# A hybrid MLA and NSA decoder block on one core: moving two norm chains, and holding filler work on three more engines to its place

## The chip, the core and the metric

The kernel runs on one core of a Trainium2 chip. A core has a TensorE (PE) for matmuls, VectorE (DVE), ScalarE (ACT) and GpSimd (POOL) for elementwise work, and SyncE (SP), which here issues the weight loads. Each engine takes its instructions in a fixed order, and semaphores make one wait for another. The metric is the device time of one execution in microseconds.

## The reference

One decoder layer over 512 tokens with 1024 channels, in float32. A normed and modulated `h` is multiplied with one wide matrix `w_in`, whose columns feed two attentions (multi-head latent attention, MLA, and native sparse attention, NSA) and their gates; a gated feed-forward part follows.

```python
h = rms_norm(x, norm1_gain[l]) * (1.0 + sc1) + sh1
z = h @ w_in[l]
(c_q, c_kv, k_pe, q_n, k_c, v_c, k_s, v_s, k_w, v_w,
 g_nsa, g_mla_merge, g_nsa_merge) = jnp.split(z, split_at, axis=-1)
y_mla = mla_attention(c_q, c_kv, k_pe, ...) @ w_o_mla[l]
y_nsa = nsa_attention(q_n, k_c, v_c, k_s, v_s, k_w, v_w, g_nsa, ...) @ w_o_nsa[l]
merged = jax.nn.sigmoid(g_mla_merge) * y_mla + jax.nn.sigmoid(g_nsa_merge) * y_nsa
x = x + gt1 * (merged @ w_out[l])
h2 = rms_norm(x, norm2_gain[l]) * (1.0 + sc2) + sh2
x = x + gt2 * ((jax.nn.silu(h2 @ ffn_w_gate[l]) * (h2 @ ffn_w_up[l])) @ ffn_w_down[l])
```

Two norms of the NSA part matter here:

```python
q = partial_rope(rms_norm(q, q_gain), cos_t, sin_t)               # queries, 8 heads of 64
kc = compress(k_c, cmp_pos_k, cmp_w1_k, cmp_w2_k)                 # compressed keys, 31 blocks x 2 groups
kc = partial_rope(rms_norm(kc, kc_gain), ...)
```

In the NSA scores three softmaxes are added with learned gates: over the compressed keys, over selected blocks and over a window of 256.

## The kernel before, in words

Every large product is split: a float32 matrix becomes a high part (`whi`, `hTh`, `phi`, `KH`), written by ScalarE, and the rest (`wlo`, `hTl`, `plo`, `KL`), by VectorE or GpSimd, and three matmuls make one product. A weight chunk is loaded by SP into `raw` and split into `whi` and `wlo`; `feed.prep(n)` does that for chunk n.

The stages, by the trace: the first products with `w_in` to some 65 us; the rest of `w_in` in a strict order to 152 us; NSA heads to 300; the MLA latents to 345; MLA heads to 440; then output products and the feed-forward part to the end at 871.

**The strict part.** There `Paced.strict` chains each engine's instructions in the order in which the code emits them. Generators are advanced by hand, `steps(gen, n)` one and `emit(...)` several. `cols_products(j)` (j = 0 to 11) issues the matmuls `ga` of 352 columns of `w_in`, four chunks to a set of four PSUM tiles, which `keep_cols` copies to `zA`, two on ScalarE and two on VectorE. Between them stand:
- `tq` (turn_q): turned queries, evacuated as `QS` in two halves by ScalarE and VectorE from the PSUM tile `pq`;
- `nq` (norm_rows of the queries): its first four steps sum squares into `msq`; its last step is a chain of 12 small VectorE operations of 128x32 from `msq` to `rs_n`, the reciprocal root norm of every token and head. The NSA scores are the first to read `rs_n`;
- `outs["k"]` (compress_out of the keys): the first step squares the compressed keys on ScalarE (`kcd`, `sk`), runs a chain on VectorE (`sk`, the `rq_..._kc` operations, `kcr`, `rp_kc`) and copies the result to `kcd`; the second step transposes `kcd` on TensorE; the third splits it to `KH` and `KL`;
- `blocks["v"]` (compress_blocks): transposes `ZC` on TensorE and copies them to `X` on ScalarE (three) and VectorE (one), after GpSimd has cleared a part of `X`;
- `pk` (prep_k): keys, split to `KH`/`KL`; `w1`, `w2`: the two small layers of the compression (`FS`, `hid`, `hidT`, `po`); `prep_gates`, `rope` work on GpSimd.

**The heads.** Outside of the strict part a scheduler, which simulates a timeline when the kernel is built, picks each engine's order from what the code emits. NSA works in eight units (tile t of 128 queries, group g of four heads): `nsa_scores` makes, for each head, window and compressed scores (`pw`), selected ones (`ps`), and on VectorE `cm`, `s` and the negated maxima `mn`, then exponentials on ScalarE; at its end four `s` are multiplied by `sm` on VectorE and four on GpSimd. Each `pw` needs the PSUM tile that the `mn` before it freed. `nsa_values` transposes (`pt`), splits (`phi`, `plo`) and multiplies (`av`). MLA has eight heads of the same kind.

Beside this main work stand fills, advanced by `Side.tick` through `later()`, or marked by `as_filler`: the merge gates (`gates_gen`, 88 steps in NSA: each step is three matmuls `gp`, eight steps one chunk with two `whi` and two `wlo`; two chunks are made ahead, in the strict part), `latent_stats` (`jk` on ScalarE, `kpr` on VectorE, `kB` on GpSimd), the modulation rows (`macc` on VectorE), and in the MLA stage the rest of the gates and `w_o_nsa` (`yn`, `gs`). In NSA the gates' `wlo` run on GpSimd, later on VectorE.

A wrapper `Paced` around each engine records the main line in `log`. When an engine's `pace` is positive, a fill on it must follow the main-line instruction that lies `pace` places back:

```python
if not Paced.fill:
    self.log.append(ins)
elif len(self.log) >= self.pace > 0:
    self.follow(ins, self.log[-self.pace])
```

Before the change only TensorE has a pace (16 in NSA, 24 in MLA).

Of the kernel before, what the change touches and what calls it, by code (L numbers as in the profile page):

```python
# [29 lines left out]
BRIDGE = 12  # L30
PACE_D = 16
PACE_F = 24
FILL_LEAD = 1
FILL_CUT = 2
YM_AHEAD = 1
# [81 lines left out]
def hybrid_block(ctx, tc, a, out):  # L117
# [47 lines left out]
    pe, act, dve, pool, sp = (Paced(e) for e in (nc.tensor, nc.scalar, nc.vector, nc.gpsimd, nc.sync))  # L165
# [153 lines left out]
    def steps(gen, n):  # L319
        for _ in range(n):  # L320
            if next(gen, "end") == "end":
                break
# [47 lines left out]
    def with_side(gen):  # L370
        for _ in gen:
            side.tick()
# [689 lines left out]
    rq, tq, rk, pk = rope_q(), turn_q(), rope_k(), prep_k()  # L1062
    blocks, w1, w2, outs = ({nm: f(i, nm) for i, nm in (K, V)} for f in (compress_blocks, compress_w1, compress_w2, compress_out))
    nk, nq = norm_rows(UK, 4, "k", rs_k), norm_rows(UQ, 8, "q", rs_n)

    def emit(*todo):
        for gen, n in todo:
            steps(gen, n)
# [107 lines left out]
    cols_products(1)  # L1176
    emit((w2["k"], 2), (tq, 1))
    feed.prep(18)
    steps(tq, 1)
    steps(nq, 1)  # L1180
    steps(outs["k"], 1)
    cols_products(2)
    steps(blocks["v"], 1)
    feed.prep(19)
# [37 lines left out]
    cols_products(9)  # L1222
    emit((w2["v"], 1), (pk, 1))
    feed.prep(29)
    emit((pk, 2), (w2["v"], 1))
    cols_products(10)
    steps(w2["v"], 2)
    steps(pk, 1)
# [151 lines left out]

    with tc.tile_pool(name="nat", bufs=2, side="right", reuse_waits="tile") as nat:
        pe.pace = PACE_D
        spill_src.update(pool=nat, bufs=2)
        units = [(t, g) for t in range(NT) for g in range(2)]
        states = [[] for _ in units]
        nb = lambda u: 1 + units[u][0] + 1 + min(units[u][0] + 1, 3) + 1
        stats = latent_stats(nat)
        side.start(5 * len(units) + sum(nb(u) for u in range(len(units))), (gates_gen, D_GATES), (stats, 8), (mods_gen, D_MODS))
        act.gate, dve.gate, pool.gate = act.last, dve.last, pool.last
        with_side(nsa_scores(nat, *units[0], states[0]))  # L1390
        for u in range(len(units)):
            pairs = [(nsa_values(nat, *units[u], states[u]), nb(u))]
            if u + 1 < len(units):
                pairs.append((nsa_scores(nat, *units[u + 1], states[u + 1]), 5))
            with_side(mix(*pairs))
    act.gate = dve.gate = pool.gate = None
    nsa_last = pe.log[-1]
    spill_src.clear()
    pe.pace = 0
    fill_on[0] = dve  # L1400
    tab_st.close()

# [217 lines left out]

    with tc.tile_pool(name="mat", bufs=2, side="right", reuse_waits="tile") as mat:
        pe.pace = PACE_F
        spill_src.update(pool=mat, bufs=GS_BUFS)
        sl = [[] for _ in range(NH)]
        side.start(12 * NH - 4, (chain(gates_gen, yn_gen), F_FILL), (mods_gen, F_MODS))
        with_side(mla_scores(mat, 0, qk[0], sl[0]))
        for h in range(NH):
            pairs = [(mla_values(mat, h, sl[h]), 5)]
            if h == 0:
                pairs.append((as_filler(norm_q(1)), 1))  # L1630
            if h + 1 < NH:
                pairs.append((mla_scores(mat, h + 1, qk[h + 1], sl[h + 1]), 5))
            if h + 2 < NH:
                pairs.append((mla_heads(h + 2, qk[h + 2]), 2))
            if h == NH - 1:
                y_gen = y_mla(0)
                pe.pace = PACE_Y
                pairs.append((as_filler(part(y_gen, 3)), 3))
            with_side(mix(*pairs))
        mla_last = pe.log[-1]  # L1640
        pe.pace = 0
        run(gates_gen)
        run(yn_gen)
    pe.gate = mla_last
# [403 lines left out]
```

## Time and profile before

| what | value |
|---|---|
| median of 3 runs | 871.19 us (871.17 to 871.99) |
| the profiled execution, its own time | 873.04 us |
| its span in the trace | 871.3 us |
| mean granted clock of TensorE | 0.986 of 2.4 GHz |
| TensorE busy | 844.3 us (97%) |
| VectorE busy | 674.9 us (77%) |
| ScalarE busy | 456.0 us (52%) |
| GpSimd busy | 109.3 us (13%) |
| chain of work that ended last: TensorE, VectorE | 81%, 7% |

A timeline row has the start, the busy time, the engine and line (L153 is the wrapper's line, so all rows have it), the operation, output and input tiles with their shapes, how many rows are merged, and in brackets how long the engine had been idle and who ended that. Busy times on one engine overlap a little, since the next instruction starts while one drains. The granted clock is 1.00 at 2.4 GHz and 0.50 at 1.2 GHz; a value between is a mean over a window.

### The profile page before, as it was taken

To read this page: it belongs to the slowest core of one execution; us is meant where nothing else is said; L and a number is where in the kernel's file an instruction comes from. 1 tells how busy PE (TensorE), PEld (TensorE's weight loads), DVE (VectorE), ACT (ScalarE), POOL (GpSimd) and SP (SyncE) were. 2 spreads that over 40 slices of the span, in tenths; PEclk is the share of its full clock that TensorE was granted. 3 is DMA by queue.
4 is the path that set the end of the run, shared out by engine and by line. 5 is a ranking of instruction groups with operands and counts; after the bars stand their busy time and mean duration, and the time that the engine had idled before them with its cause. 6 is when DMAs were issued, how large, how long until landed. Compare 5 with 4: busy or idle time off the path is not lost.

```text
span 871.3 us, 13969 instructions
## 1 busy us (share of the span) xinstructions
PE 844.3 (97%) x5060; PEld 745.1 (86%) x5060; DVE 674.9 (77%) x1391; ACT 456.0 (52%) x960; POOL 109.3 (13%) x199
## 2 busy tenths in 40 slices
PE   8999989799999999899999999999999999999997
PEld 8889889677877789787888889898999889988996
DVE  5878777888987478688789877986887858965875
ACT  4756635577766567664633254552466226641550
POOL 0007400534441013112200000000000000000000
PEclk9999989699999999999999999999999999999999
DMA  9934546343201124334697753443233313332312
GB/s 310 364 115 150 156 137 175 100 117 97 76 24 58 45 84 125 111 96 164 181 324 249 255 159 104 141 146 97 73 98 121 123 50 115 104 125 91 98 49 97
DMA packets 95705, 115.54 MB, mean 133 GB/s; under 512 B 6564, under 2 KB 68884, under 8 KB 95636
## 3 DMA queue, kind: packets, MB, share of 16 engines
q1 hardware_dynamic: 92596, 108.32, 40.1%
q10 hardware_dynamic: 2400, 4.23, 1.3%
q0 software_dynamic: 640, 2.10, 0.6%
q8 instruction: 40, 0.66, 0.3%
q14 instruction: 29, 0.24, 0.1%
HBM read 106.24 MB, written 8.39 MB: 132 GB/s over the span
## 4 chain that ended last, share of the span: by engine, by line
PE 81%; DVE 7%; ACT 3%; issue 3%; POOL 2%; DMA 2%; SPq 1%; ACTq 0%; DVEq 0%; POOLq 0%
PE d L153 14%; PE fx L153 12%; PE fy L153 9%; PE gp L153 8%; PE pt L153 4%; PE ga L153 4%; PE av L153 3%; PE yn L153 3%; PE gwo L153 3%; PE fg L153 3%; PE gym L153 3%; PE fu L153 3%; PE wo L153 3%; PE gq L153 2%; PE ps L153 2%
## 5 line engine op out<-in xcount | busy, mean ns | idle before, releaser
L153 ACT ACTIVATE whi<-raw 128x1024 fp32r<-128x1024 f32 (+4 forms) x159 | 141.1, 905 | 128.9 <-PE d L153 48.2
L153 DVE TENSOR_TENSOR wlo<-raw,whi 128x1024 fp32r<-128x1024 f32 (+4 forms) x140 | 150.9, 1086 | 56.4 <-ACT whi L153 52.4
L153 PE MATMUL d<-wlo,mh 128*128 128x512 f32 (+1 forms) x180 | 70.2, 390 | 0.0
L153 PE MATMUL d<-whi,mh 128*128 128x512 f32 (+1 forms) x180 | 69.6, 391 | 0.6 <-DVE tm L153 0.5
L153 ACT ACTIVATE s<-s,mn 128x384 f32<-128x384 f32 (+3 forms) x96 | 52.5, 547 | 28.4 <-DVE mn L153 28.3
L153 PE MATMUL d<-whi,ml 128*128 128x512 f32 (+1 forms) x180 | 67.3, 389 | 0.0
L153 DVE TENSOR_TENSOR plo<-pt,phi 128x512 fp32r<-128x512 f32 (+2 forms) x78 | 46.2, 602 | 17.8 <-ACT phi L153 17.5
L153 ACT ACTIVATE phi<-pt 128x512 fp32r<-128x512 f32 (+2 forms) x78 | 39.9, 524 | 29.3 <-PE pt L153 28.6
L153 PE MATMUL gp<-hTh,whi 128*128 128x512 f32 x128 | 54.5, 425 | 0.0
L153 PE MATMUL gp<-hTh,wlo 128*128 128x512 f32 x128 | 51.2, 400 | 0.0
L153 PE MATMUL gp<-hTl,whi 128*128 128x512 f32 x128 | 50.9, 398 | 0.0
L153 ACT ACTIVATE whi<-s 128x1024 fp32r<-128x1024 f32 (+1 forms) x36 | 30.1, 845 | 30.7 <-PE d L153 18.0
L153 PE MATMUL fx<-h2h,whi 128*128 128x256 f32 x144 | 41.2, 286 | 0.0
L153 PEld LDWEIGHTS d<-whi,mh 128*128 128x128 f32 x180 | 33.7, 188 | 8.8 <-DVE tm L153 1.2
L153 PE MATMUL fx<-h2h,wlo 128*128 128x256 f32 x144 | 40.9, 284 | 0.0
L153 PE MATMUL fx<-h2l,whi 128*128 128x256 f32 x144 | 40.8, 283 | 0.0
L153 PEld LDWEIGHTS d<-whi,ml 128*128 128x128 f32 x180 | 33.8, 188 | 7.7
L153 PEld LDWEIGHTS d<-wlo,mh 128*128 128x128 f32 x180 | 33.8, 188 | 7.4
L153 DVE TENSOR_TENSOR wlo<-s,whi 128x1024 fp32r<-128x1024 f32 (+1 forms) x36 | 33.7, 950 | 7.4 <-ACT whi L153 7.4
L153 PE MATMUL pt<-ident,s 128*128 128x128 f32 x232 | 37.4, 278 | 0.1
L153 PE MATMUL ga<-whi,hTh 128*128 128x352 f32 x96 | 32.8, 341 | 2.3 <-DVE zA L153 2.3
L153 PEld LDWEIGHTS pt<-ident,s 128*128 128x128 f32 x232 | 28.1, 142 | 7.4 <-issue 1.9
(433 smaller groups left out, 2668.0 us busy)
## 6 DMA issues: line engine op xcount, KB each, us to landing
raw<-in_ada_w_dram SPq DMA_DIRECT2D x23, 512.0 KB, 4.5
raw<-in_ffn_w_gate_dram SPq DMA_DIRECT2D x22, 512.0 KB, 3.8
raw<-in_ffn_w_up_dram SPq DMA_DIRECT2D x22, 512.0 KB, 4.0
raw<-in_ffn_w_down_dram SPq DMA_DIRECT2D x22, 512.0 KB, 3.8
araw<-in_ada_w_dram SPq DMA_DIRECT2D x32, 256.0 KB, 6.5
raw<-in_w_in_dram SPq DMA_DIRECT2D x16, 512.0 KB, 4.7
strip<-in_ada_w_dram SPq DMA_DIRECT2D x9, 512.0 KB, 3.8
raw<-in_w_in_dram SPq DMA_DIRECT2D x12, 352.0 KB, 4.0
```

The source lines that it names most:

```text
L153: out = call(*args, **kw)
```

## The change

It has three parts. The first step of `outs["k"]` moves ahead of the last step of `tq`. The last step of `nq` leaves that place and comes after chunk 29 is split, ahead of `cols_products(10)`. And a constant `PACE_E = 4` gives a pace to ScalarE, VectorE and GpSimd in the NSA heads, and to ScalarE and VectorE in the MLA heads.

```diff
+PACE_E = 4
@@ strict part, between cols_products(1) and cols_products(2)
     emit((w2["k"], 2), (tq, 1))
     feed.prep(18)
+    steps(outs["k"], 1)
     steps(tq, 1)
-    steps(nq, 1)
-    steps(outs["k"], 1)
     cols_products(2)
@@ between cols_products(9) and cols_products(10)
     emit((w2["v"], 1), (pk, 1))
     feed.prep(29)
-    emit((pk, 2), (w2["v"], 1))
+    emit((pk, 2), (w2["v"], 1), (nq, 1))
     cols_products(10)
@@ NSA heads
         pe.pace = PACE_D
+        act.pace = dve.pace = pool.pace = PACE_E
...
-    pe.pace = 0
+    pe.pace = act.pace = dve.pace = pool.pace = 0
@@ MLA heads
         pe.pace = PACE_F
+        act.pace = dve.pace = PACE_E
...
-        pe.pace = 0
+        pe.pace = act.pace = dve.pace = 0
```

What it does to the order of instructions is shown at three places. First VectorE in the strict part, around chunk 18. The names are those above; `X_1` is the values' `X`. Before:

```order
L153 TENSOR_TENSOR QS_790<-pq_1375,QS_790 64x4x128
L153 TENSOR_TENSOR QS_791<-pq_1375,QS_791 64x4x128
L153 TENSOR_SCALAR msq<-msq 128x32
...
L153 SCALAR_TENSOR_TENSOR rs_n<-rq_m_nq,rq_i_nq 128x32
L153 TENSOR_SCALAR sk<-sk 64x1
...
L153 SCALAR_TENSOR_TENSOR kcr<-po,sk,g_n 64x64
...
L153 COPY kcd<-kcr 64x64 x2
L153 TENSOR_TENSOR wlo<-raw,whi 128x1024
L153 COPY X_1_1456<-pt 64x511
```

and after:

```order
L154 TENSOR_TENSOR wlo<-raw,whi 128x704
L154 TENSOR_SCALAR sk<-sk 64x1
...
L154 SCALAR_TENSOR_TENSOR kcr<-po,sk,g_n 64x64
...
L154 COPY kcd<-kcr 64x64 x2
L154 TENSOR_TENSOR QS_790<-pq_1375,QS_790 64x4x128
L154 TENSOR_TENSOR QS_791<-pq_1375,QS_791 64x4x128
L154 TENSOR_TENSOR wlo<-raw,whi 128x1024
L154 COPY X_1_1441<-pt 64x511
```

The key norm stands ahead of the two `QS`, the query norm is gone from here, and the rest follows unchanged. On ScalarE the squares for `kcd` likewise move ahead of its two `QS`; TensorE's order in the strict part is the same.

Second, VectorE at the end of the strict part (`hidT` and `VC` belong to the values' compression). Before:

```order
L153 TENSOR_TENSOR kd_1832<-UK_210,rs_k 128x512
L153 COPY hidT_1834<-pt 128x128
L153 TENSOR_TENSOR wlo<-raw,whi 128x1024
L153 TENSOR_TENSOR KL<-pk_1863,KH 128x2x128 x2
L153 TENSOR_TENSOR VC<-vt_1877,VC 32x64
...
L153 COPY zA_794<-ga_1732 128x352
L153 COPY zA_796<-ga_1734 128x352
```

and after:

```order
L154 TENSOR_TENSOR kd_1817<-UK_210,rs_k 128x512
L154 COPY hidT_1819<-pt 128x128
L154 TENSOR_SCALAR msq<-msq 128x32
...
L154 SCALAR_TENSOR_TENSOR rs_n<-rq_m_nq,rq_i_nq 128x32
L154 TENSOR_TENSOR wlo<-raw,whi 128x1024
L154 TENSOR_TENSOR KL<-pk_1863,KH 128x2x128 x2
L154 TENSOR_TENSOR VC<-vt_1877,VC 32x64
...
L154 COPY zA_794<-ga_1717 128x352
L154 COPY zA_796<-ga_1719 128x352
```

The 12 operations of the query norm stand between `hidT` and the `wlo` of chunk 30.

Third, VectorE at the start of the NSA heads, from the last `zA` on. An `ISA` row with `s` is a score with its minimum, the `ISA mn` behind it reads the minimum out. Before:

```order
L153 COPY zA_796<-ga_1734 128x352
L153 SCALAR_TENSOR_TENSOR cm<-pw,rs_n,consts 128x32
L153 ISA s_1937,mn<-pw,consts,rs_n 128x128
...
L153 ISA s_1945,mn<-ps,mask,rs_n 128x128
...
L153 TENSOR_TENSOR kpr<-zA_793,g_k 128x32
L153 SCALAR_TENSOR_TENSOR macc<-raw,csil,macc 128x512
L153 TENSOR_TENSOR kpr<-zA_794,g_k 128x32
...
L153 SCALAR_TENSOR_TENSOR macc<-raw,csil,macc 128x512
L153 SCALAR_TENSOR_TENSOR cm<-pw,rs_n,consts 128x32
L153 ISA s_1951,mn<-pw,consts,rs_n 128x128
```

and after:

```order
L154 COPY zA_796<-ga_1719 128x352
L154 SCALAR_TENSOR_TENSOR cm<-pw,rs_n,consts 128x32
L154 ISA s_1937,mn<-pw,consts,rs_n 128x128
...
L154 ISA s_1945,mn<-ps,mask,rs_n 128x128
...
L154 SCALAR_TENSOR_TENSOR cm<-pw,rs_n,consts 128x32
L154 ISA s_1951,mn<-pw,consts,rs_n 128x128
...
L154 ISA s_1959,mn<-ps,mask,rs_n 128x128
...
L154 SCALAR_TENSOR_TENSOR cm<-pw,rs_n,consts 128x32
L154 ISA s_1969,mn<-pw,consts,rs_n 128x128
...
L154 TENSOR_SCALAR s_1937<-s_1937,sm 128x128
```

Before, four `kpr` and two `macc` stand between the first score and the second; after, the first four scores follow one another, and the first `macc` and `kpr` come behind the multiplications of `s`. On ScalarE four `whi` stood ahead of the first exponential; after, two of them come after the twelve exponentials of the first six scores. On GpSimd four `wlo` stood ahead of the first multiplications of `s`; after, two come behind these. TensorE's order is the same up to the sixth score; then the seventh `pw` and `ps` come after the first transposes of `s`. At the start of the MLA heads two `whi` and a `gs` no longer stand ahead of a `phi` on ScalarE, and four `wlo` no longer ahead of the first scores on VectorE. SP loads some chunks of `w_o_nsa` one place earlier. From 440 us on, all orders are as before.

## Rows read from the trace of the kernel before

**Rows 1.** The page, part 1: busy time, share, instructions of each engine, whole span.

```profile
PE 844.3 (97%) x5060; PEld 745.1 (86%) x5060; DVE 674.9 (77%) x1391; ACT 456.0 (52%) x960; POOL 109.3 (13%) x199
```

**Rows 2.** Waits of TensorE: us in total, times, longest us.

```profile
PE pw L153 <- DVE mn L153: 5.1, 4, 3.6
...
PE av L153 <- ACT phi L153: 2.8, 5, 1.6
...
PE ga L153 <- DVE zA L153: 2.3, 1, 2.3
PE pt L153 <- DVE kcd L153: 2.0, 1, 2.0
```

**Rows 3.** Windows: length, busy us (instructions) by engine, granted clock, DMA share, GB/s.

```profile
110.00:120.00 10.00, 7.71 (x34) 7.42 (x33) 6.62 (x13) 2.59 (x4) 0.00 (x0) 0.66 0.48 143
155.00:175.00 20.00, 15.59 (x61) 12.65 (x59) 16.09 (x60) 10.18 (x39) 9.43 (x13) 0.66 0.41 119
225.00:250.00 25.00, 24.72 (x121) 18.86 (x119) 23.06 (x74) 19.93 (x56) 9.19 (x12) 1.00 0.21 64
350.00:360.00 10.00, 7.70 (x40) 5.68 (x39) 7.87 (x25) 7.11 (x18) 2.54 (x7) 1.00 0.29 98
400.00:410.00 10.00, 8.66 (x42) 6.91 (x41) 7.59 (x17) 5.48 (x15) 1.89 (x2) 0.83 0.48 169
```

**Rows 4.** Timeline of VectorE, strict part: start us, busy us, instruction, count, [idle before].

```profile
101.17 1.39 DVE L153 TENSOR_TENSOR QS<-pq,QS 64x512 fp32r<-64x512 f32 x2 [0.30 <-ACT QS L153]
102.59 0.18 DVE L153 TENSOR_SCALAR msq<-msq 128x32 f32<-128x32 f32 x1
...
105.69 0.14 DVE L153 TENSOR_SCALAR sk<-sk 64x1 f32<-64x1 f32 x1
...
107.82 0.28 DVE L153 SCALAR_TENSOR_TENSOR kcr<-po,sk,g_n 64x64 f32<-64x64 f32 x1
...
108.80 0.29 DVE L153 COPY kcd<-kcr 64x64 f32<-64x64 f32 x2
...
110.25 0.69 DVE L153 COPY X<-pt 64x511 f32<-64x511 f32 x1
...
112.28 0.96 DVE L153 COPY zA<-ga 128x352 f32<-128x352 f32 x2
```

**Rows 5.** Timeline of ScalarE, strict part.

```profile
106.38 1.80 ACT L153 ACTIVATE X<-pt 64x512 f32<-64x512 f32 x3 [2.66 <-POOL X L153]
108.20 0.82 ACT L153 ACTIVATE zA<-ga 128x352 f32<-128x352 f32 x2
```

**Rows 6.** Timeline of ScalarE, last w_in part.

```profile
149.35 0.38 ACT L153 ACTIVATE KH<-pk 128x256 fp32r<-128x256 f32 x1 [0.49 <-DVE KL L153]
...
150.88 0.46 ACT L153 ACTIVATE zA<-ga 128x352 f32<-128x352 f32 x1 [0.59 <-PE ga L153]
```

**Rows 7.** Timeline of TensorE, start of the NSA heads.

```profile
152.10 0.39 PE L153 MATMUL gp<-hTh,whi 128*128 128x512 f32 x1
...
159.67 0.47 PE L153 MATMUL pw<-KH,QS 128*128 128x160 f32 x1 [3.56 <-DVE mn L153]
```

**Rows 8.** Timeline of VectorE, start of the NSA heads.

```profile
153.44 0.80 DVE L153 TENSOR_TENSOR kpr<-zA,g_k 128x32 f32<-128x32 f32 x1
154.16 1.83 DVE L153 SCALAR_TENSOR_TENSOR macc<-raw,csil,macc 128x512 f32<-128x512 f32 x1
...
158.35 0.74 DVE L153 SCALAR_TENSOR_TENSOR macc<-raw,csil,macc 128x512 f32<-128x512 f32 x1
159.01 0.24 DVE L153 SCALAR_TENSOR_TENSOR cm<-pw,rs_n,consts 128x32 f32<-128x32 f32 x1
...
159.72 0.07 DVE L153 DVE_READ_ACCUMULATOR2_ANT mn<- 128x1 f32 x1
...
168.80 1.01 DVE L153 TENSOR_SCALAR s<-s,sm 128x128 f32<-128x128 f32 x4
```

**Rows 9.** Timeline of GpSimd, start of the NSA heads.

```profile
152.89 5.49 POOL L153 TENSOR_TENSOR wlo<-raw,whi 128x512 fp32r<-128x512 f32 x4 [46.55 <-DVE zA L153]
```

## The prediction, made before the changed kernel ran

> **What bounds the kernel now.** I read the page's busy shares first: TensorE is busy for 97% of the span [rows 1], so only its stops and its slow stretches can be won. The list of TensorE's waits [rows 2] has stops at three places. In the strict part it waits 2.0 us for `kcd` and 2.3 us for `zA`, once each. At the start of the NSA heads one `pw` waits 3.6 us for `mn`. The waits of `av` for `phi` sum to 2.8 us and lie mostly in the MLA heads. Then the windows [rows 3]: the granted clock averages 0.66 over 110 to 120 us, which is 6.8 us at half rate, and 0.66 over 155 to 175 us, which is 13.6 us at half. Both begin at stops. In 350 to 360 us TensorE stops for 2.3 us and keeps the full clock; in 400 to 410 it stops for 1.3 us and has 0.83. So a stop of this size may or may not cost the clock. I treat the clock as a term of its own.
>
> **Strict part.** Nothing is added or removed; 12 operations (the query norm, from `msq` at 102.59 to `sk` at 105.69, 3.10 us) leave VectorE's queue here, and the key norm (105.69 to the end of `kcd` at some 109.0, 3.3 us) moves ahead of the two `QS` copies [rows 4]. These edits issue no DMA, so no queue of transfers is passed.
> The key norm can then start where `QS` began to wait, 101.17 − 0.30 = 100.87. Its `kcr` came 107.82 + 0.28 − 105.69 = 2.41 us after its start, so it will be done at 103.28, and `kcd` at 104.2. TensorE asks for `kcd` at 107.2 (its 2.0 us wait ended just past 109.0), so that wait goes. There is a small new one: the transposes of the values' blocks now take the PSUM bank that `kcr` frees, where they took the one that `QS` freed at 102.56. That is 0.7 us later, and TensorE reaches `kcd` at 107.9.
> What is late next is ScalarE's `zA`. It stands behind three `X` copies, which wait for GpSimd until 106.38 and end at 108.18; the first `zA` ends near 108.6 [rows 5]. So TensorE stops for 0.7 to 0.9 us there. VectorE's own `X` waits for the same ScalarE copies. Before, `X` began at 110.25 and `zA` at 112.28, 2.03 us later [rows 4]; after, `X` begins at 108.2 and `zA` at 110.23. The matmuls behind that `zA` start **2.05 us earlier**. The gain cannot be the 4.3 us of the two waits, since `X` is not moved.
> The clock: of 6.8 us at half rate at most 2.3 lie in the stop, so at least 4.5 are matmuls that lose half, 2.25 to 3.4 us. I price it at **2.5 us if the clock stays up**. The new stops (0.7, 0.9, 0.7) are shorter but lie closer together.
>
> **Start of the NSA heads.** The query norm's 3.10 us now stand on VectorE ahead of the last `wlo`. ScalarE's second `KH` waited for VectorE's `KL` [rows 6]; VectorE had 0.43 us to spare there, so `KH` moves from 149.35 to about 152.0. From there to the first `zA` ScalarE needs 150.88 − 0.59 − 149.35 = 0.94 us plus 0.46 for the copy: 153.4. The first gate matmul, at 152.10 before [rows 7], waits for that `zA`: a **new stop of 1.3 us** (bounds: 0, if the norm fits in other pauses, and 3.1, all of it).
> TensorE ran from 152.10 to its stop at 159.67 − 3.56 = 156.11, 4.0 us; the same work now ends at 157.4. Before, four `kpr` and two `macc` lay between VectorE's first and second score, from 153.44 to 159.01, 5.57 us [rows 8]. They are fills, and the pace moves them behind later scores; a score itself takes 159.79 − 159.01 = 0.78 us. The second score now ends as soon as TensorE delivers it, at about 157.9, and the third starts there instead of at 159.67.
> From 159.67 to the multiplications of `s` (168.80) it took 9.1 us for the scores up to the seventh, with two `macc` among them. After, the seventh score stands behind the multiplications, and the `macc` are gone. At half clock I take 8.0 us: 165.9, a gain of 2.9. At full clock a score takes 0.78 us on VectorE and some 0.4 on TensorE, since each `pw` waits for the `mn` before: four of them 4.8, and the row of small sums 0.7, 163.4, a gain of 5.4. Full clock also gives 1.8 us from 168.8 to 172.5, the rest of the 13.6 us at half. The seventh score is only put off and costs 0.4 later. So **2.5 us if the clock still falls, 6.8 if it doesn't**.
>
> **The put-off fills.** The 5.57 us of `kpr` and `macc` must be done later. VectorE is busy for 23.06 of 25 us in 225 to 250 [rows 3], and there a fill can come ahead of a score again. Ends: 0 if every one finds a pause, 5.57 if all of them show on TensorE. In that window TensorE stopped for only 0.28 us although VectorE was 92% full, so I stay near the low end: **−1.2 us**.
> The rows say how these fills are priced: the `macc` of 154.16 took 1.83 us while GpSimd ran its four `wlo`, until 158.38 [rows 9], and that of 158.35 took 0.74. The Trainium skill, page "SBUF — State Buffer", section "Who interferes with whom", has a rule for it: a VectorE instruction with two SBUF inputs contends with a GpSimd instruction that reads SBUF, and the one that starts first blocks the other. The trace agrees (1.83 against 0.74). By it the fills would shrink once they no longer lie beside those `wlo`, the term would be nearer −0.6 and the forecast 0.6 us lower; but the same `wlo` now run beside other work, and I leave it.
>
> **MLA heads.** ScalarE's weight copies and a `gs` no longer stand ahead of a `phi`, and VectorE's four `wlo` go from before the first scores. At stake: stops of 2.3 us in 350 to 360, and in 400 to 410 stops of 1.3 us and 1.7 us by the clock (17% of ten), 5.3 us in all. Bounds 0 and 5.3; the fills have to go somewhere here as well, with TensorE's `yn` matmuls behind them, so I take **+1.5 us**. From 440 us on, the order is as before: 0.
>
> **The sum.** Without the clock: 2.05 + 2.5 + 1.5 − 1.2 = 4.85 us. The clock's two terms are 2.5 and 4.3; I expect one of the two stretches to stay up, and take their mean, 3.4. That gives 8.25 us. The profiled execution took 873.04 us by its own time (span 871.3), so 864.8 on that scale; the median of the runs was 871.19, 1.85 lower, and there it is **862.9 us**.
>
> **Rivals.**
> *Both slow stretches remain* (chance 0.25). The stops shrink but TensorE is still idle between scores, and the clock fell in 400 to 410 us after only 1.3 us of stops [rows 3]. Then 4.85 us: 866.3. The Trainium skill, page "TensorE: Matmul & The Clock Gate", Part 1, says that the throttled clock is the default and that activity releases it; sparse scores would then stay slow, which is this rival. The trace bears it out only half: 350 to 360 us, with 2.3 us of stops, kept its clock.
> *Both stay up, and most MLA stops close* (0.20): 2.05 + 2.5 + 6.8 + 1.5 − 1.2 = 11.65 with the MLA term as it is, 859.5; with 5 us of it, 856.0.
> *Slower* (0.12). Held fills starve the gate matmuls. Each gate chunk needs two `wlo` on GpSimd, 2 × 1.37 = 2.74 us [rows 9]. Before, four of them ran ahead of anything else; now GpSimd first does four multiplications of `s`, and a later chunk's third matmul stands behind a `wlo` that was made just before. Nine of the eleven chunks are made in this stage. If each costs half of its pair, 1.3 us, that is 11.7 us: 871.19 − 8.25 + 11.7 = 874.6. It decides from 8.25 / 9 = 0.92 us a chunk. For it: VectorE is 92% full. Against: GpSimd is busy for only 9.19 of 25 us [rows 3], and the list of waits has none of a gate matmul.
> *The pace does little* (0.08). It fixes only the order; if the chip has each fill where it would have waited anyway, the strict part is left, 2.05 less the new 1.3, with or without 2.5 for the clock: 868 to 870.5.
>
> **How the numbers follow.** The forecast (860.5 to 865.5 by its own bounds) has 0.35. Faster by over 0.2%, 869.45 or less: the forecast, the first two rivals and half of the last, 0.35 + 0.25 + 0.20 + 0.04 = 0.84. Within 0.2%, about what a measurement of this kernel can tell from no change: the other half of the last, 0.04. Slower: 0.12. The range leaves out the slower rival, part of the last, and what lies under 856.0: 856.0 to 869.5.
>
> **What would show it.** In the trace after: no wait for `kcd`; a wait of about 0.8 us for ScalarE's `zA` and one as long for VectorE's, with matmuls again at 110.8. The first gate matmul near 153.4 less what the strict part gave, after a stop of 1.3 us. No fill between the first six scores, and the multiplications of `s` 3 to 5.5 us earlier against the first gate matmul's old place. A clock of 1.00 in one of the windows of 110 to 120 and 155 to 175. Wrong would be: a `kcd` wait that stays (the key norm is not what binds), a stop at the first gate matmul above 3 us, or waits of gate matmuls for `wlo` between 175 and 300 us.

## The result, and the profile after

The changed kernel takes **879.24 us** (median of 5 runs, 876.31 to 881.78) against 871.19 (870.21 to 872.02): a ratio of 1.009, 95% interval 1.006 to 1.012. The forecast was 862.9 us with a range to 869.5; the time lies 10 us above the range, and the sign is the other one. The profiled execution took 879.24 us by its own time, its span is 877.5.

The page's part 1 answers [rows 1]:

```profile
PE 845.0 (96%) x5060; PEld 740.7 (84%) x5060; DVE 674.7 (77%) x1391; ACT 455.3 (52%) x960; POOL 108.2 (12%) x199
```

No engine has more work than before. TensorE is busy for 845.0 us where it was for 844.3, so of the 6.2 us by which the span grew 5.5 are idle time. The list of TensorE's waits (us in total, times, longest us) answers [rows 2]:

```profile
PE av L154 <- DVE plo L154: 4.6, 7, 2.3
PE pw L154 <- DVE mn L154: 3.5, 6, 1.1
...
PE av L154 <- ACT phi L154: 2.7, 5, 1.5
PE pm L154 <- DVE macc L154: 1.9, 1, 1.9
PE pt L154 <- DVE kcr L154: 1.2, 1, 1.2
...
PE ga L154 <- DVE zA L154: 0.9, 1, 0.9
```

The waits that the change was aimed at went: no `kcd`, the `pw` wait of 3.6 us, `zA` down from 2.3 to 0.9. Two have come up, of `av` for `plo` (0.2 us before) and of `pm` for `macc` (not in the list before), and a smaller one of 1.2 us for `kcr`. Windows of the changed kernel (length, busy us by engine PE, PEld, DVE, ACT, POOL, granted clock, DMA share, GB/s) show where they lie:

```profile
100.00:120.00 20.00, 17.80 (x112) 16.86 (x111) 16.25 (x39) 9.55 (x19) 5.88 (x17) 1.00 0.45 134
152.00:175.00 23.00, 21.65 (x120) 17.07 (x119) 18.00 (x81) 18.11 (x64) 8.75 (x13) 1.00 0.14 46
...
200.00:225.00 25.00, 24.26 (x109) 18.11 (x107) 18.19 (x50) 15.74 (x46) 10.48 (x15) 0.93 0.27 74
...
275.00:300.00 25.00, 22.04 (x104) 16.20 (x103) 13.95 (x20) 11.53 (x22) 3.71 (x5) 0.93 0.13 43
...
425.00:440.00 15.00, 12.78 (x55) 10.16 (x54) 14.32 (x26) 9.05 (x18) 3.99 (x5) 0.89 0.65 213
440.00:470.00 30.00, 27.45 (x129) 22.01 (x128) 25.70 (x40) 9.71 (x14) 1.28 (x1) 1.00 1.04 384
```

Both slow stretches of [rows 3] run at 1.00 now, and three new ones stand at 200 to 225, 275 to 300 and 425 to 440 us. TensorE is idle for 3.0 us in 275 to 300, for 2.2 in 425 to 440 and for 2.6 in 440 to 470. The last two windows in the kernel before:

```profile
425.00:440.00 15.00, 14.55 (x77) 11.87 (x77) 11.67 (x26) 8.71 (x20) 3.73 (x5) 1.00 0.73 244
440.00:470.00 30.00, 30.00 (x141) 24.59 (x140) 26.22 (x41) 10.44 (x15) 1.28 (x1) 1.00 0.91 309
```

A table of marks tells the stages apart. A mark is the start of one main-line matmul in a profiled execution, here as its distance in us from the same matmul of before. The 61st `ga` stands ahead of every change of the order, so its row is what the start of that one execution added or took; read the others against it. The last `ga` ends the strict part, the 5th and 15th `pw` lie at the start of NSA, the 92nd `av` at its end, the 140th at three quarters of the MLA heads, the 156th at their end, then the last `gym` (the product with `w_o_mla`) and the last `fu` (the feed-forward part's second product). e1 to e18 are experiments, told of below.

| mark, us before | after | e1 moves only | e13 NSA, VectorE | e14 NSA, ScalarE | e4 MLA hold | e6 MLA, ScalarE | e7 MLA, VectorE |
|---|---|---|---|---|---|---|---|
| 61st `ga`, 100.6 | +0.1 | +0.3 | +0.1 | +0.2 | +1.3 | +1.1 | +0.2 |
| last `ga`, 151.9 | −4.2 | −3.9 | −4.2 | −4.1 | −3.0 | −3.2 | −4.1 |
| 5th `pw`, 159.7 | −7.1 | −3.5 | −7.2 | −7.0 | −2.5 | −2.9 | −3.6 |
| 15th `pw`, 168.3 | −8.6 | −4.5 | −7.8 | −8.9 | −3.5 | −3.8 | −3.6 |
| 92nd `av`, 296.9 | +1.6 | −4.6 | −5.8 | +3.1 | −1.1 | −1.6 | −3.8 |
| 140th `av`, 425.6 | −3.1 | −6.8 | −7.8 | +1.4 | −6.1 | −3.0 | −7.4 |
| 156th `av`, 442.0 | +0.6 | −6.7 | −7.6 | +1.5 | −2.1 | +1.7 | −1.6 |
| last `gym`, 461.7 | +3.5 | −6.7 | −7.6 | +1.5 | +4.4 | +3.9 | −1.6 |
| last `fu`, 559.4 | +6.5 | −6.8 | −7.6 | +1.9 | +7.3 | +4.8 | −1.2 |

So the changed kernel leads by 8.6 us at 168 us. It gives back 10.2 by the end of NSA, wins 4.7 in three quarters of the MLA heads, and loses 9.6 from there to the feed-forward part. From the 92nd `av` on TensorE has as many matmuls behind it at each mark in every kernel (within 0.5%), so a lead there is time and not work put off. How far one execution's mark can be trusted shows in e1, e4, e6, e7, e8 and e15: their orders are the same to the end of NSA, and from the last `ga` to the 92nd `av` they took 144.0 to 146.8 us, the longest three with a clock of 0.77 in 150 to 180 us, the others with 0.83 to 0.89. So a difference of under 3 us in that stage can be the clock's alone.

**The gain at the front.** TensorE's stops in the strict part and at the first gate matmul, after:

```profile
103.88 0.66 PE L154 MATMUL pt<-ident,ZC 128*128 128x128 f32 x4 [1.16 <-DVE kcr L154]
...
108.72 0.43 PE L154 MATMUL ga<-whi,hTh 128*128 128x352 f32 x1 [0.17 <-ACT zA L154]
...
110.83 0.43 PE L154 MATMUL ga<-whi,hTh 128*128 128x352 f32 x1 [0.87 <-DVE zA L154]
...
148.58 0.50 PE L154 MATMUL gp<-hTh,whi 128*128 128x512 f32 x1 [0.47 <-ACT zA L154]
```

VectorE after it, where the second score and the multiplications of `s` stand:

```profile
151.83 0.25 DVE L154 SCALAR_TENSOR_TENSOR cm<-pw,rs_n,consts 128x32 f32<-128x32 f32 x1 [1.98 <-PE pw L154]
...
158.09 1.03 DVE L154 TENSOR_SCALAR s<-s,sm 128x128 f32<-128x128 f32 x4
```

The second score was at 159.01 and `s` at 168.80 [rows 8]; no fill lies between now, VectorE waits 1.98 us for TensorE's `pw`, and TensorE's longest stop for VectorE's `mn` here is 0.57 us.

**The loss in NSA** lies at two places. At the end of a unit TensorE has no gate matmul to fill with: between the fourth chunk's last `gp` and the fifth's first it had none for 4.0 us before and 9.8 after, and from the 89th `gp` to the 97th the lead falls from 13.3 to 6.1 us. TensorE's rows between the 24th `gp` of the fourth chunk and the next `gp`, 10 us later, and GpSimd there:

```profile
193.73 0.39 PE L154 MATMUL gp<-hTh,wlo 128*128 128x512 f32 x1
...
198.90 0.46 PE L154 MATMUL pw<-KH,QS 128*128 128x416 f32 x1 [1.11 <-DVE mn L154]
...
203.88 0.51 PE L154 MATMUL gp<-hTh,whi 128*128 128x512 f32 x1
...
199.09 1.94 POOL L154 TENSOR_SCALAR s<-s,sm 128x256 f32<-128x256 f32 x4 [12.72 <-DVE sm L154]
...
201.91 2.52 POOL L154 TENSOR_TENSOR wlo<-raw,whi 128x512 fp32r<-128x512 f32 x2
```

At the end of NSA the held splits come in a heap, ahead of the main line, and from the 81st `av` to the 85th a lead of 2.8 us becomes a lag of 1.4. ScalarE, VectorE and TensorE there:

```profile
282.99 3.13 ACT L154 ACTIVATE whi<-raw 128x512 fp32r<-128x512 f32 x5
286.02 1.06 ACT L154 ACTIVATE phi<-pt 128x512 fp32r<-128x512 f32 x2
...
285.11 3.51 DVE L154 TENSOR_TENSOR wlo<-raw,whi 128x1024 fp32r<-128x1024 f32 x3 [2.78 <-ACT whi L154]
288.66 1.29 DVE L154 TENSOR_TENSOR plo<-pt,phi 128x512 fp32r<-128x512 f32 x2
...
289.40 0.67 PE L154 MATMUL av<-plo,V 128*128 128x512 f32 x1 [2.25 <-DVE plo L154]
```

VectorE waits 2.78 us for ScalarE's five `whi`, makes three `wlo`, and TensorE's `av` waits 2.25 us for the `plo` behind them.

**The loss at 425 to 470 us.** Two things are other than before here. The first is late loads. SP's loads of `w_o_mla` into `raw` (count, then ns of the issue, then first and last start in us), of before and of after:

```profile
L153 SPq DMA_DIRECT2D raw<-in_w_o_mla_dram x4: 367/368/384, 358.9 to 403.0; - x4
```

```profile
L154 SPq DMA_DIRECT2D raw<-in_w_o_mla_dram x4: 368/368/384, 394.6 to 429.6; - x4
```

A load needs one of the four `raw` buffers, and a buffer comes free when the chunk in it is split. The splits are what the pace holds. The loads start 36 us later and the traffic is bunched: 384 GB/s in 440 to 470 us against 309. Rows of after, of TensorE, ScalarE, VectorE and TensorE again:

```profile
431.21 0.38 PE L154 MATMUL av<-phi,VM 128*128 128x256 f32 x1 [1.52 <-ACT phi L154]
...
432.33 2.94 ACT L154 ACTIVATE whi<-raw 128x1024 fp32r<-128x1024 f32 x3
...
433.77 3.48 DVE L154 TENSOR_TENSOR wlo<-raw,whi 128x1024 fp32r<-128x1024 f32 x3
...
450.34 3.11 DVE L154 SCALAR_TENSOR_TENSOR macc<-raw,csil,macc 128x512 f32<-128x512 f32 x4 [1.10 <-DMA raw<-in_ada_w_dram]
...
453.50 1.05 PE L154 MATMUL pm<-ones,macc 128*128 128x1 f32 x8 [1.90 <-DVE macc L154]
```

The splits come in a heap here too, and the `macc` wait for their rows of `ada_w`, which use the same buffers.

The second is the order. The text ahead of the prediction says that from 440 us on all orders are as before; in the profiled executions they are not. After, the eight `pm` of the row at 453.50 stand behind 48 of the 96 `gym` matmuls, and their `macc` ahead of VectorE's work on `gym`. Before, two stood behind 84 `gym` and six behind all 96, and TensorE did not stop for them:

```profile
458.99 0.28 PE L153 MATMUL pm<-ones,macc 128*128 128x1 f32 x2
...
461.97 0.72 PE L153 MATMUL pm<-ones,macc 128*128 128x1 f32 x6
```

SP's loads of `ada_w` and `w_out` are in another order too, and so are `gwo` and `wo` on TensorE up to 506 us and some of the feed-forward part behind them.

### The profile page after: what moved, and what is told of

Same layout as the page of the kernel before. It is cut to its first block, busy times and chain, and to the rows that moved or that the text cites. A ratio compares the mean times of both kernels' runs of the same rounds, so it can differ in the third digit from the quotient of the medians.

```text
span 877.5 us, 13934 instructions
## 1 busy us (share of the span) xinstructions
PE 845.0 (96%) x5060; PEld 740.7 (84%) x5060; DVE 674.7 (77%) x1391; ACT 455.3 (52%) x960; POOL 108.2 (12%) x199
## 4 chain that ended last, share of the span: by engine, by line
PE 72%; DVE 12%; DMA 5%; issue 4%; ACT 3%; POOL 2%; SPq 1%; ACTq 0%; DVEq 0%; POOLq 0%
PE d L154 14%; PE fx L154 12%; PE gp L154 9%; PE fy L154 9%; PE pt L154 4%; PE av L154 3%; DVE s L154 3%; PE fg L154 3%; PE wo L154 3%; PE fu L154 2%; PE gq L154 2%; PE ga L154 2%; PE ps L154 2%; PE wa L154 2%; DMA yn<-spill 1%
## 5 line engine op out<-in xcount | busy, mean ns | idle before, releaser
L154 PE MATMUL gp<-hTh,wlo 128*128 128x512 f32 x128 | 51.4, 402 | 0.0
L154 PE MATMUL pt<-ident,s 128*128 128x128 f32 x232 | 39.6, 284 | 1.5 <-DVE s L154 1.1
L154 POOL TENSOR_SCALAR s<-s,sm 128x512 f32<-128x512 f32 (+3 forms) x40 | 23.8, 610 | 132.0 <-DVE sm L154 77.2
```

What stands on the lines that cost most here:

```text
L154: out = call(*args, **kw)
```

## The experiments

Diffs are against the changed kernel unless it says otherwise. Times are medians, with the ratio to the kernel before (whose medians were 870.9 to 872.2 in the five sets) and its 95% interval. What a part costs beside e1 is the difference of the two ratios times 871.

### Which part gains and which loses

**e1: the two moves without any pace.**

```diff
-        act.pace = dve.pace = pool.pace = PACE_E
...
-        act.pace = dve.pace = PACE_E
```

> The two moves of the strict part alone, with none of the new holds. All theories agree that the moves are the good part: the trace of the change has the last matmul of the strict part 4.2 us earlier than before and the first gate matmul 3.5 us earlier. The fills between the first and the second score stay as they were. Expected 866 to 868.5 us; at 870 or above, the moves would be part of what is wrong. The difference to the change (879.24) is then the cost of the holds, some 11 to 13 us.

868.4 us, 0.9958 (0.994 to 0.9975). The moves gain 3.7 us, so the paces cost 11.5.

**e3: the moves and the pace in NSA only** (three engines).

```diff
-        act.pace = dve.pace = PACE_E
```

> The moves and the holds of the NSA heads, no new hold in the MLA heads. Theory M (the MLA hold puts macc off, whose loads then fall together with those after 440 us and cost the 5.6 us that the change loses from 437 to 560): 873 to 875 us. If the NSA holds alone leave the macc late, the time stays at 878 to 881 us.

871.99 us, 1.0001 (0.9983 to 1.0018): the NSA pace costs 3.7 us.

**e4: the moves and the pace in the MLA heads only.**

```diff
-        act.pace = dve.pace = pool.pace = PACE_E
```

> The moves and the hold of the MLA heads, no new hold in the NSA heads. Theory M: the moves alone plus some 4 to 5 us after 440, 871 to 873 us. If the MLA hold is harmless or takes its stops away, as the prediction had it, 865 to 868 us, at or under the moves alone.

877.0 us, 1.0053 (1.0025 to 1.0081): the MLA pace costs 8.3 us. The two costs add up to 12.0, close to the 11.5 of both.

**e2: the changed kernel without GpSimd's pace.**

```diff
-        act.pace = dve.pace = pool.pace = PACE_E
+        act.pace = dve.pace = PACE_E
```

> The whole change, but GpSimd is not held in the NSA heads (ScalarE and VectorE are). Theory G (GpSimd's hold keeps the gates' wlo behind the next unit's multiplications, so that gate matmuls are missing where TensorE waits for scores): most of the 14 us that the change loses between 175 and 295 us come back, 866 to 870 us, and GpSimd's long idle stretches (12.7 us before 199) end with a wlo. Theory V (the put-off kpr and macc on VectorE and the late whi on ScalarE are the cost): no more than 2 us come back, 877 to 880 us.

881.07 us, 1.0102 (1.0069 to 1.0135). Freeing GpSimd gives nothing back, so the held `wlo` of my slower rival are not the cause.

**e13 and e14: the moves and the pace in NSA on one engine**, VectorE or ScalarE; no pace in MLA.

```diff
-        act.pace = dve.pace = pool.pace = PACE_E
+        dve.pace = PACE_E
...
-        act.pace = dve.pace = PACE_E
```

> The moves and a hold of VectorE alone in the NSA heads (pace 4). Both engines and GpSimd held gave 872.0, none 868.4. If the put-off kpr and macc on VectorE are the cost of the NSA hold, 871 to 873 us. If ScalarE's held whi are (raw buffers come back late), 867 to 869.5 us, perhaps with the early gain of the first unit kept.

> The moves and a hold of ScalarE alone in the NSA heads (pace 4), with VectorE and GpSimd free. If ScalarE's held whi are the cost, 871 to 873 us, with the loads of w_in and w_q_b in 170 to 290 us as late as with all three held; if VectorE's kpr and macc are, 867 to 869.5 us.

e13: **863.84 us, 0.991 (0.9887 to 0.9933)**, faster than both kernels. e14 (with `act.pace` in that place): 876.3 us, 1.0054 (1.0034 to 1.0073). The two engines have opposite signs: VectorE's pace gains 4.2 us beside e1, ScalarE's costs 8.4. By the marks, both lead by 7 us at the 5th `pw`; e14 loses 12 from the 15th to the end of NSA, 7.3 of it between the 89th and the 97th `gp` and 4.2 between the 81st and the 85th `av`, the two places of the changed kernel. Waits of TensorE in e13, beside those of after above:

```profile
PE av L154 <- ACT phi L154: 2.6, 5, 1.6
PE pw L154 <- DVE mn L154: 2.1, 4, 0.6
...
PE av L154 <- DVE plo L154: 1.2, 2, 1.0
```

**e6 and e7: the moves and the pace in MLA on one engine**, ScalarE or VectorE; no pace in NSA.

```diff
-        act.pace = dve.pace = pool.pace = PACE_E
...
-        act.pace = dve.pace = PACE_E
+        act.pace = PACE_E
```

> The moves and a hold of ScalarE alone in the MLA heads (pace 4). Theory R: a weight chunk's raw buffer is given back only after its wlo, which needs its whi; holding whi is enough to put the loads of w_o_mla and ada_w off (358.9 and 378.5 us before, 391.8 and 400.0 with both engines held), so the cost of the MLA hold is there in the main, 873 to 877 us. Theory V (VectorE gets too much work late in the MLA heads because its own fills are held): VectorE is free here, 867 to 870 us.

> The moves and a hold of VectorE alone in the MLA heads (pace 4). Theory R and theory V both expect most of the cost here, 873 to 877 us, since the wlo that give the raw buffers back are on VectorE; the trace is to show the loads of w_o_mla after 385 us. At 869 or less both would be wrong, and ScalarE's order would be what costs.

e6: 878.01 us, 1.0084 (1.0058 to 1.011). e7 (`dve.pace`): 871.38, 1.0003 (0.9989 to 1.0016). Both cost, ScalarE's 11 us beside e1, VectorE's 3.9. Both load late, from 391.3 and 390.8 us on. From the end of NSA to the end e7 loses 2.3 us and e6 6.3, and the marks show where they part: between the 140th and the 156th `av` both lose (e7 5.8, e6 4.7); from there to the last `fu` e6 loses 3.1 and e7 0.4. Up to 505 us e7 has the order of before there, and e6 has its eight `pm` early, as after.

### The two moves apart

**e11: the query norm's move alone**, and **e12: the key norm's move alone**; no pace in either. Against the kernel before:

```diff
-    steps(nq, 1)
     steps(outs["k"], 1)
     cols_products(2)
...
-    emit((pk, 2), (w2["v"], 1))
+    emit((pk, 2), (w2["v"], 1), (nq, 1))
```

```diff
+    steps(outs["k"], 1)
     steps(tq, 1)
     steps(nq, 1)
-    steps(outs["k"], 1)
     cols_products(2)
```

> Before, with the query norm moved behind chunk 29 and the key norm left where it was; no holds. My sum gave the 2.05 us to the earlier X and zA on VectorE, which need the query norm's 3.1 us to be gone and not the key norm to be first: kcd would then be ready at 105.9, before TensorE asks for it at 107.2, and the transposes of the values' blocks need not wait for kcr. If that is right, 867 to 869 us, as good as both moves. If the key norm's place matters, 870 to 872 us.

> Before, with the key norm moved ahead of the two QS and the query norm left behind them, where it was; no holds. The wait for kcd goes, but X and zA on VectorE come as late as before, so TensorE should stop for them instead: 870.5 to 872.5 us, no measurable gain. If the key norm's wait was worth its 2.0 us, 868.5 to 870 us.

e11: 868.16 us, 0.9962 (0.9944 to 0.998), as good as both moves in the runs. e12: 874.43, 1.0033 (1.0016 to 1.005). The matmul behind VectorE's `zA`, in before, in e11 and in e12 (110.83 after):

```profile
112.86 0.66 PE L153 MATMUL ga<-whi,hTh 128*128 128x352 f32 x1 [2.29 <-DVE zA L153]
```

```profile
110.90 0.66 PE L153 MATMUL ga<-whi,hTh 128*128 128x352 f32 x1 [0.88 <-DVE zA L153]
```

```profile
112.50 0.66 PE L153 MATMUL ga<-whi,hTh 128*128 128x352 f32 x1 [2.73 <-DVE zA L153]
```

Taking the query norm out of VectorE's queue moves it by 2 us; the key norm's place moves it by 0.4. The clock is another matter. From the 61st `ga` to the last it took 51.4 us before, 47.1 to 47.2 in all fourteen traces with both moves, 48.6 in e11 and 50.2 in e12, and over 110 to 120 us the clock was 0.66, 1.00, 0.83 and 0.83. Why e12 is slower than before by 2.9 us in its runs isn't settled: its profiled execution was the fastest of its ten, and that of before ended 0.2 us later.

**e16: the query norm ahead of `prep_gates`**, the key norm in its old place, no pace. Against the kernel before:

```diff
     steps(w2["v"], 1)
+    steps(nq, 1)
     run(prep_gates())
```

> Before, with the query norm alone moved, to just ahead of the step that turns the NSA gates into sigmoids, where VectorE waits 2.1 us for ScalarE in the trace of the moves; no holds. If the new stop ahead of the first gate matmul came from the norm's place late in the strict part, it shrinks from 1.3 us to 0.3 or less and the time is about 1 us under that of the query norm's move alone, 866.5 to 867.8 us. If the place makes no difference, 867.8 to 869 us.

867.95 us, 0.9962 (0.9947 to 0.9976). The strict part ends 3.35 us earlier and the first gate matmul starts 3.35 earlier, so the stop at the first gate matmul is gone. That stop was worth 0.6 us in e1 and after, and the runs can't tell e16 from e11.

### What in the pace costs

**e5: no pace, but fills of ScalarE and VectorE in NSA follow the first unit's four scores** (`floor` is the last instruction of these on each engine).

```diff
+            if Paced.fill and self.floor is not None:
+                self.follow(ins, self.floor)
...
-        act.pace = dve.pace = pool.pace = PACE_E
...
+        first = nsa_scores(nat, *units[0], states[0])
+        steps(first, 4)
+        act.floor = act.last
+        dve.floor = dve.last
...
-        act.pace = dve.pace = PACE_E
```

> The moves, no pace on ScalarE, VectorE or GpSimd; instead every fill on ScalarE and VectorE in the NSA heads has to follow the first unit's four scores on its engine, and is free from there on. This keeps the order that gave the change its 8 us at the start of the heads (first multiplications of s, gate matmul 60), without holding anything later. If the hold further on is what costs (theory R: held fills keep the four raw buffers, so the loads behind them come late), 861 to 865 us, 4 to 7 under the moves alone. If the put-off kpr, macc and whi themselves cost what they gave, 867 to 870 us.

867.42 us, 0.9956 (0.9941 to 0.9972), no better than e1, though the 5th `pw` comes 6.7 us early as in e13. So a gain at the start of NSA is not kept by itself (of 6.7 us at the 5th `pw` 3.9 are left at the 92nd `av`); with e13's pace all through NSA more of it stays.

**e8: the moves and the MLA pace at 16 places back instead of 4.**

```diff
-        act.pace = dve.pace = pool.pace = PACE_E
...
-        act.pace = dve.pace = PACE_E
+        act.pace = dve.pace = 16
```

> The moves and a hold of ScalarE and VectorE in the MLA heads with pace 16 where the change has 4, so that a fill may come sixteen main-line instructions early. Theory R: loads move back towards their old places, and the time lies between the moves alone (868.4) and pace 4 (877.0), 869 to 873 us. If any hold costs the same (an effect of the order's mere change), 875 to 878 us.

873.94 us, 1.0023 (1.0008 to 1.0038): the cost beside e1 falls from 8.3 to 5.7 us, and the first load of `w_o_mla` is at 382.2 instead of 391.8. It loses 3.6 us between the 140th and the 156th `av` and 0.4 from there to the last `fu`; its order up to 505 us is that of before.

**e9: the changed kernel, with the splits of weight chunks free of the pace. e10: with the `macc` free too.**

```diff
-            elif len(self.log) >= self.pace > 0:
+            elif len(self.log) >= self.pace > 0 and not Paced.free:
...
+        Paced.free = True
         for i in range(cut):
             c = slice(i * m, (i + 1) * m)
             hi_of(h[:, c], raw[:, c])
             lo_of(l[:, c], raw[:, c], h[:, c], eng_lo)
+        Paced.free = False
```

> The whole change, but the whi and wlo of weight chunks are not held; every other fill (kpr, jk, kB, macc, gs, the second norm of the MLA queries) is. Theory R (the cost comes through the raw buffers: a held whi or wlo gives its buffer back late, so the loads behind it come late and bunch): most of the 10.8 us between the moves alone (868.4) and the change (879.2) go, 868 to 872 us, and the first loads of w_o_mla are back before 370 us. macc reads raw buffers too and is still held in the NSA heads, so some cost may stay. Theory O (the other held fills, or any forced order, cost it): 876 to 880 us.

> The same, and macc not held either, so that nothing which reads a raw buffer is held. Theory R: 867 to 870 us, the time of the moves alone, whatever happens to kpr, jk and gs. Theory O: 876 us or more.

e9: 874.41 us (without one execution of 2874 us, which is the one that was profiled, so its trace is not read for times), 1.0034 (1.0013 to 1.0055). e10: 879.05, 1.0072 (1.0048 to 1.0096). In e10 `w_o_mla` loads from 365.2 us on, the order up to 505 us is that of before again, and from the end of NSA to the end nothing is lost (+6.4 to +6.1 us). But NSA itself is worse than after (+6.4 against +1.6 at the 92nd `av`).

**e15: the moves and the MLA pace, chunk splits free** (e4 with the edit of e9).

> The moves and the MLA hold of ScalarE and VectorE, but the whi and wlo of weight chunks are not held; no hold in the NSA heads. With them held it was 877.0. Theory R for the MLA heads: the cost is gone, 866.5 to 869.5 us, and w_o_mla is loaded before 370 us. If other held fills (gs, the second query norm, the first output step) cost it, 872 us or more.

872.09 us, 1.0002 (0.9988 to 1.0016). Freeing the splits gives back some 4.4 of e4's 8.3 us. The loads are where e1 has them, the order from the last `av` on is that of before, and in the profiled execution (span 866.6, the fastest of its ten) the stretch from the last `av` on loses nothing (−4.5 to −4.6). First e1, then e15:

```profile
L154 SPq DMA_DIRECT2D raw<-in_w_o_mla_dram x4: 367/368/384, 354.2 to 397.6; - x4
```

```profile
L155 SPq DMA_DIRECT2D raw<-in_w_o_mla_dram x4: 367/368/368, 354.8 to 398.7; - x4
```

**e18: the moves and the NSA pace of ScalarE and VectorE, chunk splits free** (e3 without GpSimd, with the edit of e9).

> The moves and a hold of ScalarE and VectorE in the NSA heads, but not of the weight chunks' whi (their wlo are on GpSimd there and are not held either); no hold in the MLA heads. If the late whi are what ScalarE's hold costs (theory R), the time comes near that of VectorE's hold alone, 863 to 866 us, and the loads of w_in come by 205 us as there. If jk and gs are it (gs gives back the PSUM tile of a gate chunk), 871 to 876 us.

872.66 us, 1.0019 (1.0001 to 1.0037), no better than e3. By the marks the splits do count at one of the two places: between the 81st and the 85th `av`, where after, e2, e3 and e14 lose 4.2 us each, e18 loses nothing, and nor does e10, the other trace with free splits in NSA. But e18 loses as much elsewhere: its fifth chunk still comes 6.6 us behind the fourth (4.0 in e1 and e13), and from the 121st `gp` to the 145th a lead of 4.8 becomes a lag of 1.0. The other fills on ScalarE are `gs`, which empties the PSUM tile of a finished gate chunk, and `jk`. `gs` is late: the last `gp` of the seventh chunk and its `gs`, first in e13, then after.

```profile
232.83 0.40 PE L154 MATMUL gp<-hTh,wlo 128*128 128x512 f32 x1
...
234.10 0.59 ACT L154 ACTIVATE gs<-gp 128x512 f32<-128x512 f32 x1
```

```profile
235.86 0.39 PE L154 MATMUL gp<-hTh,wlo 128*128 128x512 f32 x1
...
247.57 0.59 ACT L154 ACTIVATE gs<-gp 128x512 f32<-128x512 f32 x1
```

0.9 us against 11.3 (11.6 in e14). But little is lost there: from the 161st `gp` to the 169th, on both sides of that `gs`, the lead falls by 1.5 us after and by 1.7 in e14. No run took `gs` or `jk` alone out of the pace, so which of ScalarE's held fills leaves TensorE without gate matmuls behind the fourth chunk stays open.

**e17: e16 with VectorE's pace in NSA**, to see if two gains add up.

> The version that the runs so far point to: before, with the query norm moved ahead of the NSA gates' step, the key norm left in its place, and a hold of VectorE alone in the NSA heads (pace 4). If the parts add up, 4.6 us of the hold (868.4 to 863.8) under the 868.0 of the query norm at that place: 862.5 to 864.5 us, and under 0.993 of before. If the hold's gain needed the moves' exact order, 866 to 868 us.

887.93 us, 1.02 (1.0172 to 1.0227), the slowest of all. At the end of the MLA heads it led by 1.7 us; by the last `fu` it was 14.1 behind. It has no pace in MLA, yet it loads `w_o_mla` from 391.4 us and `w_out` only from 465.9 (e1: 440.8), and TensorE's list of waits has

```profile
PE pm L153 <- DVE macc L153: 5.0, 1, 5.0
PE gwo L153 <- ACT whi L153: 3.3, 1, 3.3
```

So late loads and a changed order come with a loss at the same place without a pace in MLA: there the scheduler that orders all engines came out so by itself.

## Why the prediction was wrong, step by step

**Strict part: right.** `kcd` gone, stops of 1.16, 0.17 and 0.87 us, matmuls again at 110.83 where 110.8 was worked out. That is 2.03 us of the 2.05, and from the 61st `ga` to the last 4.3 us are won, so the clock gave 2.2 of the 2.5. The 2.03 come from the query norm alone (e11 against e12). For the clock's part the traces have both moves at 1.00 fourteen times of fourteen and the query norm's move alone once of three (e16, not e11 and e17); the runs of e1 and e11 show no difference.

**The stop at the first gate matmul: half.** The row shows 0.47 us idle, the marks 0.6; 1.3 was taken, with 0 as the low bound.

**Start of the NSA heads: right, at the upper end.** The multiplications of `s` start at 158.09 where it was 168.80, 10.7 us earlier, and 4.2 of these are the strict part's. The other 6.5 stand against the 2.9 (clock falls) and 5.4 (it stays) that were worked out for this point; 0.8 of the difference is the shorter stop. Without the pace (e1) the fills are still there; TensorE's stop and VectorE's multiplications in e1:

```profile
156.16 0.31 PE L154 MATMUL pw<-KH,QS 128*128 128x160 f32 x1 [3.10 <-DVE mn L154]
...
164.32 1.01 DVE L154 TENSOR_SCALAR s<-s,sm 128x128 f32<-128x128 f32 x4
```

So some 6 us of that lead (164.32 − 158.09) come from the pace, with the clock that fell in e1 (0.81 in 160 to 170 us) and not after. That the clock would stay up was a guess, and it could not have been more: after and e13 have the same three stops here (0.21, 0.57 and 0.57 us, the last before 157.7), and the clock stays in the one and falls in the other. Windows of after, then of e13:

```profile
156.00:160.00 4.00, 2.99 (x22) 2.60 (x22) 3.69 (x24) 3.56 (x13) 1.94 (x5) 1.00 0.01 4
160.00:164.00 4.00, 4.00 (x22) 2.86 (x22) 3.14 (x11) 4.00 (x16) 2.13 (x2) 1.00 0.32 89
```

```profile
156.00:160.00 4.00, 3.01 (x16) 2.40 (x17) 3.82 (x24) 2.90 (x11) 1.58 (x4) 0.85 0.41 119
160.00:164.00 4.00, 4.00 (x13) 3.03 (x12) 2.08 (x6) 3.91 (x13) 2.51 (x2) 0.50 0.02 2
```

The Trainium skill, page "TensorE: Matmul & The Clock Gate", section "Part 1: The HAM clock gate", makes the clock a matter of how active the engine has just been, which was the ground of the rival with both stretches slow. These two kernels, with 2.99 and 3.01 us busy in the same four, came out on either side; the rows of the profile do not tell which way it goes.

**The put-off fills, −1.2: the step that failed first.** It priced the fills of VectorE that were moved from the start, and for VectorE the size may stand: e13 gives back 2.0 of its 7.8 us by the end of NSA, no more than the clock alone can do there. But the pace holds *every* fill of three engines all through NSA, and ScalarE's stood at nothing in the sum, without a reason. Holding them costs 8.4 us in the runs (e14 against e1) and the whole lead by the end of NSA, at the two places shown above.

**MLA heads, +1.5: right for three quarters, then not.** After wins 4.7 us to the 140th `av` (e1 2.2, so 2.5 are the pace's), then loses 3.7 to the end of the heads.

**From 440 us on, 0: wrong.** Its ground was that the order there is as before, and that is not so: the `pm` at 453.50 stand early. And an order alone would not have said when a buffer is free: the held splits keep `raw`, and the loads come 36 us late.

The traces of after and of all experiments but e9 sort by these two. Where `w_o_mla` is first loaded at 382 us or later (after, e2, e4, e6, e7, e8, e17), 3.6 to 5.8 us are lost from the 140th `av` to the 156th; where by 365, at most 1.1. The heap of splits comes with the late loads (two or three `wlo` in a row in each of the seven, one at a time in e1 and e15), so the runs don't tell which of the two TensorE stops for. From the 156th `av` to the last `fu`, after, e2, e4, e6 and e17, with another order up to 505 us, lose 5.9, 9.8, 9.4, 3.1 and 15.8 us; with the order of before, e7's and e8's late loads among them, it is 2.0 at most. Where the splits are freed, the loads and that order are back (e10, e15). That the scheduler puts the `pm` elsewhere because the buffers come late in its timeline is argued: e7 and e8 load late and keep the order. And e15's runs are still 3.8 us above e1's; its trace, of the fastest of its ten, does not show where. A fifth `raw` buffer would test the part of the loads; no run has one. The Trainium skill, page "Perfetto Trace Analysis", section "Optimization Strategy", has a gap that repeats as a possible sign of too few buffers for the next tile. Here the number of buffers is the one with which e1 runs well, and what changed is how long a chunk keeps one.

**The slower rival** had the sign and the kind (held fills starve the gate matmuls, 874.6 us), but put it on GpSimd's `wlo`. e2 says no: with GpSimd free it is 881.07. The list of waits has no `gp` that waits for `wlo`, which the prediction named as the sign of it; TensorE's order simply has other work where a `gp` would stand, so a lack of fills shows as waits of `pw` and `av`.

## What to carry to other kernels

Work that is put off also puts off what it gives back: a buffer, a PSUM tile, and with them a load that starts tens of microseconds later; so compare the order to the very end of the program, and then ask of each held instruction what it frees and who waits for that. Hold one engine at a time: here the same rule gained 4 us on VectorE and cost 8 on ScalarE, and together with the two moves they gave the time of before (e3). An early lead is worth what is left of it at the end of the stage, and two gains needn't add up where a scheduler decides the whole order anew (e13 and e16 gained, e17 lost 16 us).

## What the runs showed of the hardware

The clock held at 1.00 through stops of 1.16, 0.17 and 0.87 us within some 8 us in the strict part, where it had averaged 0.66 behind stops of 2.0 and 2.3 [rows 2, 3]. At the start of NSA the same three short stops left it at 1.00 in one kernel and at 0.50 for four microseconds in another (after and e13, above), and e13 is the faster of the two by 15 us: the clock decided little here. Up to 148 us every engine has the same order in e16 and e17, and TensorE stops for 1.20 and 0.87 us in the one, 1.21 and 0.87 in the other; over 110 to 120 us the clock was 1.00 in e16 and 0.83 in e17, and from the 61st `ga` to the last e17 took 1.3 us longer. So the same order can come out on either side. The DMA engines were at a share of 1.04, as the profile counts it, in 440 to 470 us after (384 GB/s), and there the `macc` waited for their rows; before, at 0.91 and 309 GB/s, TensorE was busy for all of these 30 us.
